# A decoder layer on one core: input also as columns, weights as blocks of 4 KB rows, token scale behind the products

## The chip, the cores and the metric

The kernel runs on one core of a Trainium2 chip. The metric is the device time in microseconds (us). The engines are TensorE (PE; PEld is its weight load), VectorE (DVE), ScalarE (ACT), GpSimd (POOL) and SyncE (SP), which here only issues transfers. L12 is line 12 of the kernel file; the changed kernel has line numbers of its own.

## The reference

One decoder layer, batch 1, S = 256 tokens, width D = 1024, in float32. Cut to what matters here:

```
h    = rms_norm(x, norm1_g)                  # x * rsqrt(mean(x*x) + 1e-6) * g, per token
proj = h @ w_in                              # 1024 x 5408: RWKV, attention, two gates
z    = z_rwkv + mu * (shift_right(z_rwkv) - z_rwkv)
y_a  = rwkv7_time_mix(z, ...)                # 8 heads of 64
y_b  = moba_attention(q, k, v)               # 8 heads of 64, causal here (one block of 256)
x    = x + (sigmoid(g_a) * (y_a @ w_branch_a) + sigmoid(g_b) * (y_b @ w_branch_b)) @ w_out
h2   = rms_norm(x, norm2_g)
x    = x + conv_ffn(h2, ...)                 # up 1024 x 5632, conv of width 3, GELU, down 2816 x 1024
```

The norm's factor per token, rs = rsqrt(mean(x*x) + 1e-6), is a scalar for each token. So it can be applied to x before a product with a weight, or to the product behind it.

## The kernel before, in words

**Products.** Every weight and every activation is split in two halves of a shorter format: hi is the rounded value (a cast), lo the rest (a subtraction). A product is the sum hi*hi + hi*lo + lo*hi, so each weight block of 1024 columns per partition makes three sets of products on PE. A block (128 x 1024 float32, 512 KB) is loaded into `raw` by SP (L254), cast to `whi` by ACT (L266), and subtracted into `wlo` by DVE (L276). There are 4 `raw`, 4 `whi` and 3 `wlo` buffers, and the next block's transfer is issued behind the subtraction that frees a `raw`. In `wst` (L304, L306, L309) the weights stand still and 256 tokens move; in `xst` (L325, L326, L329) activations stand still and 512 weight columns move.

**Order.** The first stage, `first_steps`, is written out by hand: within it each engine's instructions stand in the order of the code. The rest comes from two threads, `chain` (the RWKV recurrence) and `bulk` (projections: k, r, q, v, gates, branches), and later `att`; a loop by costs and latencies weaves them, and a scheduler sets each engine's order when the program is built. Every engine then works strictly in that order.

**First stage.** x is loaded by tokens (L85, four pieces of 256 KB). For tokens 0 to 127 (t = 0) ACT squares and sums (L415), a root (L422) and a reciprocal (L423) give rs, and DVE scales x (L434) before it is turned. Tokens 128 to 255 (t = 1) are turned unscaled. PE turns 16 squares of 128 x 128 (L427) into the PSUM tiles `xt`; ACT makes the upper halves times the gain (L446, `hh`), DVE the lower (L449, `hl`). The small vectors come as rows of 128 and are turned as well (L438, L149, L159). The first product takes blocks 0 and 1 of `w_in` (48 products, L489, tile `idle`, named after the warming products of L396 that stand in the same bank). Behind them r1 (rs of t = 1) is spread and turned (L508) into `rbc`, a 128 x 128 tile with the same row in each partition. `tl` (L515) is a narrow product with 32 columns, in four column groups, in plain float32.

**Behind the first stage.** `second(p)` (L369) multiplies the half of a product that belongs to t = 1 by `rbc`. `shift` mixes a token with the one ahead (ACT L372, then DVE L373). The chain goes on with `fold` (L595), the sigmoids of L607, a scan and exponentials; then it needs k, and later r and v. `num` scales the attention's parts of t = 1 by r1.

Of the kernel before, what the change touches and what calls it, by code (L numbers as in the profile page):

```python
# [18 lines left out]
S = 256  # L19
# [14 lines left out]
NEG = -3.0e38  # L34


def body(tc, x, positions, norm1_g, w_in, rwkv_mu, w_decay_up, decay_bias, w_aaa_up,
         aaa_bias, w_gate_up, k_k, k_a, r_k, ln_g, ln_b, q_norm_g, k_norm_g, w_branch_a,
         w_branch_b, w_out, norm2_g, w_up, conv_w, conv_b, w_down, out):
# [3 lines left out]
    with ctx:  # L43
# [45 lines left out]
        def rows(ap, n):  # L89
            return ap.rearrange("o d -> (o d)").rearrange("(n c) -> n c", c=128)  # L90


        p0 = t1("p0", (8, 128))
        p1 = t1("p1", (43, 128))
        p2 = t1("p2", (96, 128))
        mu1 = rwkv_mu[0]
        rk1 = r_k[0].rearrange("h n -> (h n)").rearrange("(n c) -> n c", c=128)

        x_sb = load_x((nc.sync, nc.sync))
        nc.scalar.dma_start(p0, rows(norm1_g, 8))  # L100
# [36 lines left out]
        par = cst.tile([128, 51], F32, name="par")  # L137
# [5 lines left out]
        rbc = cst.tile([128, 128], F32, name="rbc")  # L143
        r1 = rs[:, 1:2]

        pts = []

        def params_turned():
            pe.transpose(pts[0][:, 0:43], p1, ident[:43, :43])  # L149

        def late_params():
            pt = pts[0]
            dve.tensor_copy(par[:, 8:51], pt[:, 0:43])
# [3 lines left out]
        def mlp_params():  # L157
            pt = atp("pt")
            pe.transpose(pt[:, 0:96], p2, ident[:96, :96])  # L159
            dve.tensor_copy(cpar, pt[:, 0:96])  # L160
# [11 lines left out]
        loads, at_ = [], 0  # L172
        for r, n in ((mu1[0:1792].rearrange("(n c) -> n c", c=128), 14),
                     (rows(decay_bias, 4), 4), (rows(aaa_bias, 4), 4), (rows(k_k, 4), 4), (rows(k_a, 4), 4),
                     (rk1, 4), (rows(ln_g, 4), 4), (rows(ln_b, 4), 4)):
            loads.append((p1[at_:at_ + n], r))
            at_ += n
            if at_ == 14:
                loads.append((p1[14:15].rearrange("o (g c) -> o g c", g=4),
                              bass.AP(tensor=mu1.tensor, offset=mu1.offset + 1792, ap=[[0, 1], [0, 4], [1, 32]])))  # L180
                at_ += 1
        loads += [(wdu[0:64], w_decay_up[0]), (wdu[64:128], w_aaa_up[0]),

                  (wgu, w_gate_up[0, 0:128])]
        loads += [(wgt[32 * g:32 * g + 32], w_gate_up[0, 128:160, 128 * g:128 * g + 128]) for g in range(4)]
        for i, g in enumerate((q_norm_g, k_norm_g)):
            loads.append((gqk[:, i], bass.AP(tensor=g.tensor, offset=g.offset, ap=[[0, 128], [1, 64]])))
        gcol = cst.tile([128, 2], F32, name="gcol")
        gl = [(gcol[64 * q:64 * q + 64, i:i + 1], bass.AP(tensor=g.tensor, offset=g.offset, ap=[[1, 64], [1, 1]]))
              for i, g in enumerate((q_norm_g, k_norm_g)) for q in range(2)]  # L190
        loads.append((posi, positions[0].rearrange("(t p) -> p t", p=128)))
        loads += [(p2[0:66], conv_w[0].rearrange("w (n c) -> (w n) c", c=128)), (p2[66:88], rows(conv_b, 22)),
                  (p2[88:96], rows(norm2_g, 8))]

        def small_loads(n):
            for _ in range(n):
                nc.gpsimd.dma_start(*loads.pop(0))
# [1251 lines left out]
```

## Time and profile before

| | |
|---|---|
| three runs | 403.39, 404.11, 404.26 us (median 404.11) |
| profiled execution | 404.9 us, with a span of 403.1 us from the first to the last instruction |
| PE busy | 398.0 us, 3282 instructions |
| DVE busy | 321.8 us, 554 instructions |
| ACT busy | 234.7 us, 396 instructions |
| POOL busy | 44.4 us, 76 instructions |
| HBM read | 68.37 MB, 173 GB/s over the span with what is written |
| DMA packets | 60194, of which 50506 under 2 KB |

A busy share is an average over stages. In what follows a timeline row gives start, length, engine, line, operation, tiles and count, and in brackets the idle time before it and what ended it. A row of windows gives for one stretch the busy time and the count of each engine, the clock that the throttle granted by its records, and what the DMA moved. A chain row gives start and length of a piece of the chain that ended last.

### The profile page before, as it was taken

What the parts mean: (1) busy time and instruction counts of PE and PEld (TensorE: products, weight loads), DVE (VectorE), ACT (ScalarE), POOL (GpSimd) and SP (SyncE); (2) the same over time, 40 slices, a digit from 0 to 9 for tenths busy, and PEclk for the clock granted to TensorE, in tenths of its full rate; (3) what the DMA queues carried; (4) which work ended last, traced back from release to release, by engine and by line L of the source; (5) the groups of instructions that cost most, each with busy time, mean ns of one, the idle gap of its engine ahead of it and who ended that gap; (6) DMA issues with size and microseconds to landing.
All of it is one profiled execution on the core that took longest, in us unless ns stands there. A gap on an engine that the chain in (4) does not pass through costs nothing.

```text
span 403.1 us, 8318 instructions
## 1 busy us (share of the span) xinstructions
PE 398.0 (99%) x3282; PEld 347.9 (86%) x3282; DVE 321.8 (80%) x554; ACT 234.7 (58%) x396; POOL 44.4 (11%) x76
## 2 busy tenths in 40 slices
PE   8999999999999999999999999999999999999996
PEld 5899899888899898999888888888888888888885
DVE  4798999989667897688876897977869779687694
ACT  6899766366555795454564764545546446355450
POOL 7600505213410011100000000000000000000000
PEclk9999999999999999999999999999999999999999
DMA  7983556746844335536664657565665665656612
GB/s 246 299 269 82 138 157 210 205 132 146 224 124 142 106 88 155 167 123 206 201 179 141 210 167 232 165 206 182 198 202 167 209 193 171 209 180 198 195 54 106
DMA packets 60194, 70.36 MB, mean 175 GB/s; under 512 B 7608, under 2 KB 50506, under 8 KB 60154
## 3 DMA queue, kind: packets, MB, share of 16 engines
q1 hardware_dynamic: 59222, 69.40, 57.0%
q0 software_dynamic: 880, 0.41, 0.6%
q8 instruction: 26, 0.43, 0.5%
q14 instruction: 14, 0.11, 0.1%
q10 hardware_dynamic: 52, 0.01, 0.0%
HBM read 68.37 MB, written 1.44 MB: 173 GB/s over the span
## 4 chain that ended last, share of the span: by engine, by line
PE 98%; DMA 1%; SPq 0%; DVE 0%; issue 0%
PE acc L1330 20%; PE acc L1335 10%; PE acc L304 9%; PE acc L306 8%; PE acc L309 8%; PE acc L325 5%; PE acc L329 5%; PE acc L326 5%; PE f L1352 5%; PE f L1350 5%; PE f L1354 5%; PE idle L489 2%; PE pgr L715 1%; PE xt L427 1%; DMA x<-in_x_dram 1%; PE ppt L1155 1%
## 5 line engine op out<-in xcount | busy, mean ns | idle before, releaser
L266 ACT CAST whi<-raw 128x1024 fp32r<-128x1024 f32 x122 | 127.8, 1051 | 111.6 <-PE acc L1330 41.2
L276 DVE TENSOR_TENSOR wlo<-raw,whi 128x1024 fp32r<-128x1024 f32 x122 | 148.3, 1218 | 37.0 <-PE acc L1335 14.0
L1330 PE MATMUL acc<-hx,whi 128*128 128x512 f32 x352 | 89.5, 395 | 0.0
L1330 PEld LDWEIGHTS acc<-hx,whi 128*128 128x128 f32 x352 | 63.4, 188 | 12.4
L304 PE MATMUL acc<-hx,whi 128*128 128x256 f32 x224 | 56.3, 287 | 0.0
L306 PE MATMUL acc<-hx,whi 128*128 128x256 f32 x224 | 54.1, 278 | 0.0
L1335 PEld LDWEIGHTS acc<-hx,wlo 128*128 128x128 f32 x352 | 46.8, 188 | 4.0
L1335 PE MATMUL acc<-hx,wlo 128*128 128x256 f32 x352 | 47.3, 277 | 0.0
L304 PEld LDWEIGHTS acc<-hx,whi 128*128 128x128 f32 x224 | 42.1, 188 | 2.5 <-issue 1.4
L306 PEld LDWEIGHTS acc<-hx,whi 128*128 128x128 f32 x224 | 42.1, 188 | 0.1
L309 PE MATMUL acc<-hx,wlo 128*128 128x256 f32 x224 | 34.6, 276 | 0.0
L1352 PE MATMUL f<-whi,hb 128*128 128x512 f32 x80 | 31.2, 390 | 0.0
L1354 PE MATMUL f<-wlo,hb 128*128 128x512 f32 x80 | 31.2, 390 | 0.0
L1350 PE MATMUL f<-whi,hb 128*128 128x512 f32 x80 | 31.2, 389 | 0.0
L309 PEld LDWEIGHTS acc<-hx,wlo 128*128 128x128 f32 x224 | 29.6, 188 | 0.0
L1340 DVE TENSOR_REDUCE an<-acc 128x256 f32<-128x512 f32 x22 | 14.2, 686 | 9.4 <-PE acc L1335 9.3
L325 PE MATMUL acc<-whi,hx 128*128 128x512 f32 x48 | 19.4, 405 | 0.0
L326 PE MATMUL acc<-whi,hx 128*128 128x512 f32 x48 | 18.8, 391 | 0.0
L1354 PEld LDWEIGHTS f<-wlo,hb 128*128 128x128 f32 x80 | 15.0, 188 | 3.2
L1352 PEld LDWEIGHTS f<-whi,hb 128*128 128x128 f32 x80 | 15.0, 188 | 2.8
L1350 PEld LDWEIGHTS f<-whi,hb 128*128 128x128 f32 x80 | 15.0, 188 | 2.8
L329 PE MATMUL acc<-wlo,hx 128*128 128x512 f32 x48 | 14.9, 392 | 0.0
(341 smaller groups left out, 635.1 us busy)
## 6 DMA issues: line engine op xcount, KB each, us to landing
raw<-in_w_ffn_up_dram SPq DMA_DIRECT2D x44, 512.0 KB, 4.4
raw<-in_w_in_dram SPq DMA_DIRECT2D x41, 512.0 KB, 4.1
raw<-in_w_ffn_down_dram SPq DMA_DIRECT2D x22, 512.0 KB, 3.3
raw<-in_w_out_dram SPq DMA_DIRECT2D x8, 512.0 KB, 3.9
x<-in_x_dram SPq DMA_DIRECT2D x8, 256.0 KB, 4.2
raw<-in_w_branch_b_dram SPq DMA_DIRECT2D x4, 512.0 KB, 4.6
raw<-in_w_branch_a_dram SPq DMA_DIRECT2D x4, 512.0 KB, 3.5
out_dram<-o SPq DMA_DIRECT2D x3, 256.0 KB
```

Source lines behind the costliest of these rows:

```text
L266: act.copy(hi[:, :k * c], raw[:, :k * c])
L276: eng.tensor_tensor(lo[:, :n], raw[:, :n], hi[:, :n].bitcast(F32), op=OP.subtract)
L304: pe.matmul(om, wh[:, k, ms], xh[:, k0 + k], start=k0 + k + m == 0, stop=False, skip_group_check=True)
L306: pe.matmul(om, wh[:, k, ms], xl[:, k0 + k], start=False, stop=False, skip_group_check=True)
L309: pe.matmul(om, wl[:, k, ms], xh[:, k0 + k], start=False, stop=k0 + k == nk - 1 and m == n - 1, skip_group_check=True)
L325: pe.matmul(ps_[t], xh[:, K, ts], wh[:, k], start=K == 0, stop=False)
L326: pe.matmul(ps_[t], xl[:, K, ts], wh[:, k], start=False, stop=False)
L1330: pe.matmul(ps_[m], wh[:, k, m * 128:m * 128 + 128], hx[:, k0 + k].rearrange("p a s -> p (a s)"), start=k0 + k == 0, stop=False, skip_grou ...
L1335: pe.matmul(ps_[m][:, 0:S], wl[:, k, m * 128:m * 128 + 128], hh[:, k0 + k], start=False, stop=k0 + k == 7, skip_group_check=True)
L1350: pe.matmul(fin[f], hb[:, 0, i, ts], wh[:, 0, cs], start=st, stop=False, skip_group_check=f == 3)
L1352: pe.matmul(fin[f], hb[:, 1, i, ts], wh[:, 0, cs], start=False, stop=False, skip_group_check=f == 3)
L1354: pe.matmul(fin[f], hb[:, 0, i, ts], wl[:, 0, cs], start=False, stop=False, skip_group_check=f == 3)
```

## The change

Inputs are laid out anew on the host, without arithmetic: the weights as `blocks`, in the order in which they are used, each 128 rows of 4 KB that lie together (before, a row of a block was 4 pieces of 1 KB, 2 of 2 KB or 1 of 4 KB of the weight matrix); x a second time as columns (`x_cols`: 128 x 8 x 256, which is x turned); the small vectors as two ready 128-partition tables (`vec1`, `vec2`), and the narrow weights in one piece each.

In the first stage x is not turned, and no token's scale is applied ahead of the products. ACT squares the columns (8 squares of 128 x 256), PE sums them over the partitions with a matrix of ones, in four column groups, and a second product with 1/(32 D) adds the groups and spreads the mean to all partitions. ACT takes the root, DVE the reciprocal; `rbc` is now 128 x 256, for all tokens. `second` covers all 256 tokens, `tls` too, and `num` scales both t. rs by tokens, for `num`, comes from turning `rbc` on PE behind `fold`. GpSimd takes half of block 1's cast as well.

```diff
-        x_sb = load_x((nc.sync, nc.sync))
-        nc.scalar.dma_start(p0, rows(norm1_g, 8))
+        nc.scalar.dma_start(par, vec1)
+        xc = [b4("xc", (128, 4, S)) for _ in range(2)]
+        for ks in (slice(0, 2), slice(2, 4)):
+            nc.sync.dma_start(xc[0][:, ks], x_cols[:, ks])
...
-                for ks in ((slice(0, 2), slice(2, 4)) if first else (slice(0, k),)):
-                    nc.sync.dma_start(rv[:, ks], ap[:, ks])
+                for cs in ((slice(0, 512), slice(512, 1024)) if first else (slice(0, 1024),)):
+                    nc.sync.dma_start(raw[:, cs], blocks[i, :, cs])
...
-            v = p.rearrange("p (m c) -> p m c", m=2)[:, :, 128:256]
-            dve.tensor_tensor(v, v, rbc[:, None, :].to_broadcast([128, 2, 128]), op=OP.mult)
+            v = p.rearrange("p (m c) -> p m c", m=2)
+            dve.tensor_tensor(v, v, rbc[:, None, :].to_broadcast([128, 2, S]), op=OP.mult)
...
-            for k in range(4):
-                turn(1, k)
-            pt = bk[5][:, 256:264]
-            pe.transpose(pt, p0, ident[:8, :8])
-            dve.tensor_copy(par[:, 0:8], pt)
-            for k in (0, 1, 2, 3, 4, 6, 7, 5):
-                turn(0, k)
-            for k in (4, 6, 7, 5):
-                turn(1, k)
+            def square(k):
+                act.activation(sq[k // 4][:, k % 4], at(k), AF.Square)
...
-            for k in (0, 1, 2, 3, 4, 6, 7, 5):
+            for cs in quarters[:2]:
+                pool.tensor_copy(w[1][1][:, cs], w[1][0][:, cs])
+            lower(1, halves_[0], pool)
+            for k in range(4):
                 high(k)
-            for cs in halves_:
-                act.copy(w[1][1][:, cs], w[1][0][:, cs])
+            for k in range(4):
+                square(k)
+            for k in range(4, 8):
+                high(k)
+            act.copy(w[1][1][:, halves_[1]], w[1][0][:, halves_[1]])
+            for k in range(4, 8):
+                square(k)
...
+            first(1, 0, hh)
+            first(1, 0, hl)
+            sums = chp("sums")[:, 0:S]
+            for k in range(8):
+                g = k % 4
+                pe.matmul(sums[32 * g:32 * g + 32], tok[:, 0:32], sq[k // 4][:, k % 4], start=k < 4, stop=k >= 4,
+                          skip_group_check=True)
+            su = t1("su")
+            act.copy(su, sums)
+            first(1, 1, hh)
+            mean = chp("mean")[:, 0:S]
+            pe.matmul(mean, tok[:, 32:160], su, start=True, stop=True)
+            act.activation(rbc, mean, AF.Sqrt, bias=eps1[:, 0:1])
+            dve.reciprocal(rbc, rbc)
             act.activation(warm, eps1[:, 0:1], AF.Sigmoid)
             split_hi()
-            split_lo()
...
-            pe.transpose(pts[0][:, 128:256], rx, ident)
-            dve.tensor_copy(rbc, pts[0][:, 128:256])
...
-            dve.tensor_copy(tls[:, 0:128], tl[:, 0:128])
-            dve.tensor_tensor(tls[:, 128:256], tl[:, 128:256], rbc, op=OP.mult)
+            dve.tensor_tensor(tls, tl, rbc, op=OP.mult)
...
+            with tc.issue_after(pfi):
+                for t in range(2):
+                    pfi = pe.transpose(pft[:, S + t * 128:S + t * 128 + 128], rbc[:, t * 128:t * 128 + 128], ident).ins
+            dve.tensor_copy(rs, pft[:, S:2 * S].rearrange("p (t c) -> p t c", t=2)[:, :, 0])
```

Three places in the engines' orders, before and after. First TensorE, from behind the warming products to `tl` (`xt` are the turns, `idle` the first stage's products, `pt` small turns). Before:

```order
L427 MATMUL xt<-ident,x 128x128 x4
L438 MATMUL xt<-ident,p_69 128x8
L427 MATMUL xt<-ident,xn_168 128x128 x4
L427 MATMUL xt<-ident,xn_169 128x128 x4
L427 MATMUL xt<-ident,x 128x128 x4
L489 MATMUL idle<-hx,whi 128x256 x16
L489 MATMUL idle<-hx,wlo 128x256 x8
L149 MATMUL pt<-ident,p_70 128x43
L489 MATMUL idle<-hx,whi 128x256 x16
L489 MATMUL idle<-hx,wlo 128x256 x8
L508 MATMUL pt<-ident,rx_231 128x128
L515 MATMUL tl<-hx,wtr 32x256 x16
```

After:

```order
L410 MATMUL idle<-hx,whi 128x256 x16
L410 MATMUL idle<-hx,wlo 128x256 x8
L410 MATMUL idle<-hx,whi 128x256 x16
L425 MATMUL sums<-sq,tok 32x256 x8
L410 MATMUL idle<-hx,wlo 128x256 x8
L431 MATMUL mean<-su,tok 128x256
L441 MATMUL tl<-hx,wtr 32x256 x16
```

The turns are gone; the column sums and the mean stand among block 1's products.

Second VectorE, from the k projection's first lower half to the end of the first stage (`idle` is the first stage's product, `wlo` are lower halves). Before:

```order
L276 TENSOR_TENSOR wlo<-raw,whi 128x1024
L509 COPY rbc<-pt 128x128
L369 TENSOR_TENSOR idle<-idle,rbc 128x2x128
L373 SCALAR_TENSOR_TENSOR xwa<-idle,par,xwa 128x255
L523 COPY tls<-tl 128x128
L524 TENSOR_TENSOR tls<-tl,rbc 128x128
L373 SCALAR_TENSOR_TENSOR xg<-idle,par,xg 128x255
L276 TENSOR_TENSOR wlo<-raw,whi 128x1024
```

After:

```order
L252 TENSOR_TENSOR wlo<-raw,whi 128x1024
L433 RECIPROCAL rbc<-rbc 128x256
L317 TENSOR_TENSOR idle<-idle,rbc 128x512
L321 SCALAR_TENSOR_TENSOR xwa<-idle,par,xwa 128x255
L449 TENSOR_TENSOR tls<-tl,rbc 128x256
L321 SCALAR_TENSOR_TENSOR xg<-idle,par,xg 128x255
L252 TENSOR_TENSOR wlo<-raw,whi 128x1024 x2
```

The copy of `rbc` has become a reciprocal of 256 columns, and the rescale covers 512.

Third VectorE where k's shifts (`zk`) end and r's lower halves begin. Before:

```order
L373 SCALAR_TENSOR_TENSOR zk<-acc,par,zk 128x255
L276 TENSOR_TENSOR wlo<-raw,whi 128x1024
L373 SCALAR_TENSOR_TENSOR zk<-acc,par,zk 128x255
L369 TENSOR_TENSOR acc<-acc,rbc 128x2x128
L276 TENSOR_TENSOR wlo<-raw,whi 128x1024
```

After:

```order
L321 SCALAR_TENSOR_TENSOR zk<-acc,par,zk 128x255
L317 TENSOR_TENSOR acc<-acc,rbc 128x512
L252 TENSOR_TENSOR wlo<-raw,whi 128x1024
L321 SCALAR_TENSOR_TENSOR zk<-acc,par,zk 128x255 x2
L252 TENSOR_TENSOR wlo<-raw,whi 128x1024
```

k's second rescale (`acc<-acc,rbc`) moves ahead of the lower half of r's second block.

More of the change, by code (lines that the diff above doesn't have):

```diff
@@ L87, in load_x @@
             return xs
[L89 to L97, printed above, removed]
[L99 to L100 removed]
+        par = cst.tile([128, 51], F32, name="par")
+        nc.scalar.dma_start(par, vec1)
+        xc = [b4("xc", (128, 4, S)) for _ in range(2)]
+        for ks in (slice(0, 2), slice(2, 4)):
+            nc.sync.dma_start(xc[0][:, ks], x_cols[:, ks])
         first_low = []
@@ L142, in body @@
         rs = cst.tile([128, 2], F32, name="rs")
[L143 to L149, printed above, removed]
+        rbc = cst.tile([128, S], F32, name="rbc")
         def late_params():
-            pt = pts[0]
-            dve.tensor_copy(par[:, 8:51], pt[:, 0:43])
             dve.tensor_scalar(omm, par[:, MU:MU + 15], -1.0, 1.0, op0=OP.mult, op1=OP.add)
             dve.tensor_scalar(omka, par[:, KA:KA + 4], -1.0, 1.0, op0=OP.mult, op1=OP.add)
[L157 to L160, printed above, removed]
         def col(i):
@@ L378, in first_steps @@
         def first_steps():
-            for _ in range(2):
-                nc.scalar.dma_start(*loads.pop(0))
             for i in range(2 * NRAW):
                 load_next(i == 0, early=i >= NRAW)
+                if i == 0:
+                    nc.sync.dma_start(xc[1], x_cols[:, 4:8])
                 if i == 2:
-                    nc.sync.dma_start(wtr, win[:, :, 1792:1824])
+                    nc.sync.dma_start(wtr, w_narrow)
                 if i == 3:
-                    for _ in range(2):
-                        nc.sync.dma_start(*loads.pop(7))
+                    nc.sync.dma_start(wdu, w_two_up)
             skipped[0] = NRAW
@@ L474, in first_steps @@
                 lower(0, cs, dve)
-            lower(1, halves_[0], pool)
-            for k in (4, 6, 7):
+            for k in range(4, 8):
                 low(k)
-            square(1, 1)
-            low(5)
             lower(1, halves_[1], dve)
-            root(1)
-            rx = t1("rx1", (128, 128))
-            dve.tensor_copy(rx, r1.to_broadcast([128, 128]))
+            late_params()
             def first(b, lo_, xx, ks=(0, 1, 2, 3)):
@@ L1222, in bulk @@
             yield from proj4("k", 4)
-            for _ in range(7):
-                nc.sync.dma_start(*loads.pop(0))
+            nc.sync.dma_start(wgu, w_gate)
+            nc.sync.dma_start(wgt, w_gate_rest)
+            nc.sync.dma_start(gqk, gain_rows)
             yield from proj4("r", 0)
@@ L1243, in bulk @@
             threads.insert(1, ["att", attention(), now_t + 3.0])
-            for _ in range(3):
-                nc.sync.dma_start(*loads.pop(0))
+            nc.sync.dma_start(cpar, vec2)
             for j in range(1, 4):
@@ L1438 @@
     arrays, args = {}, []
-    for name in _INS:
-        a = np.ascontiguousarray(inputs[name])
+    for name, a in lay_out(inputs).items():
+        a = np.ascontiguousarray(a)
         arrays[f"in_{name}_dram"] = a
```

160 lines of the change are left out of this document (61 added, 99 removed).

## The prediction

> **What bounds the kernel now.** I read the page first (busy shares, the chain of waits), then TensorE's own waits, then the first 20 us engine by engine, then how far ahead of TensorE the other engines run.
>
> ```profile
> PE 398.0 (99%) x3282; PEld 347.9 (86%) x3282; DVE 321.8 (80%) x554; ACT 234.7 (58%) x396; POOL 44.4 (11%) x76
> PE 98%; DMA 1%; SPq 0%; DVE 0%; issue 0%
> PE idle L396 <- DVE eps L391: 1.5, 1, 1.5
> PE xt L427 <- DMA x<-in_x_dram: 0.4, 1, 0.4
> ```
>
> The chain that ends last is TensorE for 98% of the span, and TensorE waits twice in all: 1.5 us at the start and 0.4 us for x. So no weight transfer is ever waited for there, and what the change can give lies in the first 18 us, where TensorE works on turns, or in fewer products later (there are none). What it can take is a new wait.
>
> ```profile
> 1.46 3.60 PE L396 MATMUL idle<-ones 128*128 128x512 bf16 x8 [1.46 <-DVE eps L391]
> 5.50 1.09 PE L427 MATMUL xt<-ident,x 128*128 128x128 f32 x4 [0.45 <-DMA x<-in_x_dram]
> 6.72 1.97 PE L427 MATMUL xt<-ident,xn 128*128 128x128 f32 x8
> 9.20 2.86 PE L489 MATMUL idle<-hx,whi 128*128 128x256 f32 x16
> 11.89 1.07 PE L489 MATMUL idle<-hx,wlo 128*128 128x256 f32 x8
> 13.08 2.10 PE L489 MATMUL idle<-hx,whi 128*128 128x256 f32 x16
> 16.13 1.93 PE L515 MATMUL tl<-hx,wtr 128*32 128x256 f32 x32
> 17.99 0.38 PE L304 MATMUL acc<-hx,whi 128*128 128x256 f32 x1
> ```
>
> (Timeline of TensorE: start, length, line, tiles, count.) Turns run from 5.50 to about 9.2, the first stage's 48 products from 9.20 to 16.1, the narrow product `tl` to 18.0, then the k projection starts. Here is what makes the turns cheaper than they look:
>
> ```profile
> 9.00:10.00 1.00, 0.81 (x4) 0.88 (x5) 1.00 1.10 375
> 10.00:11.00 1.00, 1.00 (x7) 1.00 (x7) 1.00 1.22 276
> 11.00:12.00 1.00, 1.00 (x11) 1.00 (x10) 1.00 1.23 225
> 205.50 0.54 PE xt L1291 x4
> ```
>
> Of line 489 alone, 0.81 us hold 4 products before 10 us (0.20 each), 11 fit into the microsecond from 11 to 12. Four turns take 1.09 us at 5.5 and 0.54 us at 205.5 (chain of waits). TensorE thus runs at about half pace (0.21 us for 256 columns) until some 10.8 us and at 0.113 (from 8 in 1.07, whose last alone lasts about 0.28) after that, though the clock column says 1.00 throughout. The 3.7 us of turns are worth about 1.9 us at full pace.
>
> **The change part by part.**
>
> *The start of the products.* Block 0's first half stood fifth among the quarter megabytes in SP's queue; now it is third, behind two pieces of the columns.
>
> ```profile
> 1.65 3.72 DMA x<-in_x_dram
> 8.11 1.43 POOL L466 CAST whi<-raw 128x256 fp32r<-128x256 f32 x4 [1.31 <-DMA raw<-in_w_in_dram]
> 7.24 3.34 ACT L446 ACTIVATE hx<-xt,par 128x256 fp32r<-128x256 f32 x8 [0.95 <-PE xt L427]
> 10.45 1.15 ACT L470 CAST whi<-raw 128x512 fp32r<-128x512 f32 x2
> ```
>
> The third piece landed at 1.65 + 3.72 = 5.4. One GpSimd quarter (1.43/4 = 0.36, with hand-over 0.4) gives the first product at 5.8 instead of 9.2. ScalarE's upper halves cost 0.42 each as before (3.34/8) and are ready by then.
>
> *The work up to the end of the token sums.* Let M be the moment the token means stand in PSUM. TensorE has 48 products, 8 column-sum products in fp32 (half of `tl`'s 1.93: 0.96) and one fp32 product with 256 columns, priced by the fold below at 0.59. Four changes of kind cost 0.12 each, as from the end at 12.96 to the next start at 13.08: 0.5.
>
> ```profile
> 19.48 0.59 PE L595 MATMUL fold<-tls,fold 128*128 128x256 f32 x2
> ```
>
> If the pace changes at 10.8 as before: 5.0/0.21 = 24 products until then, 24 x 0.113 = 2.7 after, so M = 10.8 + 2.7 + 0.96 + 0.59 + 0.5 = 15.6. If it changes by 7.5, block 1 sets it: it lies at the same place (2 MB) in the queue as before, where the row of line 470 shows it landed by 10.45; with 1 us less than that, M is about 14.5. If it changes at 12.3: 31 products until then, 17 x 0.113 after, M = 16.3. I take 15.4, nearest the first with some weight on the early case. [...]
>
> *From the sums to the shifts.* Before, `rbc` was at hand soon after block 1; now a root and a full reciprocal precede it, on ScalarE and VectorE, and every rescale (`second`) covers 256 tokens, not 128.
>
> ```profile
> 16.23 0.29 DVE L509 COPY rbc<-pt 128x128 f32<-128x128 f32 x1 [1.26 <-PE pt L508]
> 16.56 0.43 DVE L369 TENSOR_TENSOR idle<-idle,rbc 128x256 f32<-128x256 f32 x1
> 18.43 0.45 ACT L372 ACTIVATE xg<-idle,omm 128x256 f32<-128x256 f32 x1
> 43.33 1.75 DVE L650 RECIPROCAL rq<-rq 128x256 f32<-128x256 f32 x1
> 42.89 0.41 ACT L649 ACTIVATE rq<-rq 128x256 f32<-128x256 f32 x1
> 39.03 0.68 DVE L638 TENSOR_TENSOR wgl<-wgu,wgh 128x512 fp32r<-128x512 f32 x1
> ```
>
> Old path from 16.23 to the xg shift: 2.20. New: minus the copy (0.33) plus root 0.41, reciprocal 1.75, hand-overs 0.15, and 0.68 - 0.43 = 0.25 for the wider rescale (priced by the nearest 512-wide row): 4.4. The xg shift starts at M + 4.4 = 19.8, against 18.43: 1.4 us later, although TensorE is up to 1 us ahead.
>
> *Where that delay goes.* Behind the xg shift ScalarE is full, and its next goods are upper halves.
>
> ```profile
> 20.11 0.47 ACT L372 ACTIVATE xgt<-fold,omm 128x256 f32<-128x256 f32 x1 [0.28 <-PE fold L595]
> 31.56 1.04 ACT L266 CAST whi<-raw 128x1024 fp32r<-128x1024 f32 x1
> 32.63 1.23 DVE L276 TENSOR_TENSOR wlo<-raw,whi 128x1024 fp32r<-128x1024 f32 x1 [0.46 <-ACT whi L266]
> 20.00:35.00 15.00, 15.00 (x132) 14.53 (x132) 12.43 (x37) 14.86 (x26) 0.00 (x0) 1.00 0.58 185
> 35.00:60.00 25.00, 25.00 (x175) 21.88 (x174) 24.79 (x32) 19.38 (x31) 5.85 (x14) 1.00 0.56 149
> 57.30 1.23 DVE L276 TENSOR_TENSOR wlo<-raw,whi 128x1024 fp32r<-128x1024 f32 x1
> 58.78 0.62 PE L309 MATMUL acc<-hx,wlo 128*128 128x256 f32 x4
> ```
>
> (Windows: the busy times are PE, PEld, DVE, ACT, POOL.) From 20 to 35 ScalarE is busy 14.86 of 15 us; VectorE then starts r's second lower half at 32.63, the moment the cast ends, and is busy 24.79 of 25 us until 60. At its end v's second block: lower half ready at 58.53, used at 58.78. VectorE runs 0.25 us ahead of TensorE there, the smallest lead I found anywhere. So the sum is VectorE's. The same ScalarE items as before stand between the xg shift and that cast; the old 0.28 idle before L372 goes: 1.4 - 0.28 = +1.1. In VectorE's order k's second rescale now precedes this lower half (before, it followed), so it starts some 0.1 behind the cast: +1.2. From there to v's second lower half stand the same rows, without that rescale (-0.33) and with r's two rescales wider (+0.5): +0.2. Lower half ready: 58.53 + 1.2 + 0.2 = 59.9, that is 1.15 us after TensorE used it before. In case of a gap in VectorE's run (it waits for ScalarE's shifts and the root of `rq`) up to 0.5 more; with M = 14.5, 0.25 us late; with M = 16.3, 2.0 us.
>
> Until then TensorE's lead does not help: it is spent as one wait of 1 to 2 us at v's second block.
>
> *Behind it.* The leads are larger; one of the smallest:
>
> ```profile
> 176.34 1.22 DVE L276 TENSOR_TENSOR wlo<-raw,whi 128x1024 fp32r<-128x1024 f32 x1
> 180.84 0.39 PE L309 MATMUL acc<-ybh,wlo 128*128 128x256 f32 x2
> 176.89 0.25 PE L159 MATMUL pt<-ident,p 96*128 96x96 f32 x1
> ```
>
> 180.84 - 177.56 = 3.3 us cover the wider rescales of v and the gates, 10 x 0.25 = 2.5 us over 110 us; without that cover they would cost up to 2.5. One turn (L159) goes: -0.1. The two turns of `rbc` (2 x 0.14) and the narrower small loads lie ahead of v's wait and cost nothing by themselves; without the wait they would take back 0.3. Rows of 4 KB instead of 1 KB: nothing, since TensorE waits for no weights, and 1 KB rows already moved 375 GB/s (row of 9 to 10 us).
>
> Sum: 403.1 + 1.15 - 0.1 = 404.2 of span. The profiled execution took 404.9 for 403.1, the median is 404.11, so I put the +1.05 on the median: 405.2.
>
> **The rivals.** (1) *Even*: full pace comes early, M near 14.5. VectorE then has v's half 0.25 late, less the L159 turn: +0.1, 404.2. For it: the pause before the first product (5.1 to 5.8) is short, and some 3 us of dense products follow it. Against: after a pause of 0.45 at the same place the old kernel stayed slow until 10.8. (2) *TensorE's lead survives*: VectorE is not the bound at v's block, because its stretch holds slack that I take for work, or the reciprocal lies beside a wait. Then the k projection's start counts: M + 0.2 + 1.75 = 17.3 against 17.99, +0.3 for the two turns, -0.1: -0.5 with M = 15.4, -1.4 with 14.5; 403.0 for the middle. Against it: 24.79 of 25 us. (3) *VectorE does not recover*: the wider rescales after 60 us use up the 3.3 us of lead; from the point where their sum and the 1.2 us pass it, each costs 0.25. With half of the ten uncovered: 405.2 + 1.25 = 406.5. (4) *The layout alone does nothing*: the 4 KB rows show in the DMA's landing times and nowhere else. It is part of each case.
>
> **How the numbers follow.** Forecast 0.55, with its own range 404.6 to 406.2 (M from 14.8 to 16.0 and up to 0.5 of gaps); rival 1 0.22, rival 2 0.16, rival 3 0.07. A measurement of this kernel cannot tell less than 0.2% (0.8 us) from no change. Of the forecast a quarter lies under +0.8, of rival 1 nearly all, of rival 2 a quarter: same 0.14 + 0.20 + 0.04 = 0.38; faster 0.02 + 0.12 = 0.14; slower 0.41 + 0.07 = 0.48. Range 403.5 to 406.5.
>
> **What would show it.** Right: the first product of block 0 near 5.8 at about 0.21 apart; the means' root near 15.5; a 1.75 us reciprocal right behind; the xg shift near 19.8; the cast of r's second block ending near 33.7; a wait of TensorE for VectorE's lower half near 59, 1 us or more with what k's earlier start gained, and none behind it. Wrong: no TensorE wait around 59 (rival 2), the pace doubling before 8 us (rival 1), further waits for lower halves after 70 us (rival 3), or a TensorE wait for the sums or for the first stage's data between 6 and 15 us, which I have at nothing.

## The result, and the profile after

The changed kernel took 409.88 us (median of 4 runs, 409.0 to 410.2); the kernel before took 403.89 (median of 4). The ratio is 1.0148, 95% interval 1.0132 to 1.0163: 6.0 us slower. The forecast was 405.2 with a range up to 406.5; the direction was right, the size was not. The profiled execution took 409.75 for a span of 407.66; before, it took 404.9 for 403.13. So 4.5 us of span lie between the two, and 0.3 us outside the span. The remaining 1.1 us or so is that the profiled execution of the kernel before (404.9) lay 1.0 above its own median, and that of the changed kernel 0.1 below.

The page: busy times, the chain of waits, and then TensorE's waits.

```profile
PE 399.6 (98%) x3282; PEld 348.7 (86%) x3282; DVE 327.0 (80%) x546; ACT 234.4 (58%) x395; POOL 40.2 (10%) x68
PE 79%; DVE 8%; ACT 6%; DMA 5%; issue 1%; SPq 0%; ACTq 0%; DVEq 0%
PE idle L410 <- POOL whi L384: 2.0, 1, 2.0
PE idle L343 <- DVE eps L337: 1.5, 1, 1.5
PE acc L283 <- DVE wlo L252: 0.9, 1, 0.9
```

TensorE held 98% of the chain before, now 79%: from 21.6 to 61.6 us the chain runs over ScalarE and VectorE, and what lies ahead of that is put down to transfers (5%). Two new waits stand in the list: 2.0 us for block 0's upper half, and 0.9 for a lower half. The second is v's second block, the place that the prediction named:

```profile
60.37 1.23 DVE L252 TENSOR_TENSOR wlo<-raw,whi 128x1024 fp32r<-128x1024 f32 x1
61.64 0.74 PE L283 MATMUL acc<-hx,wlo 128*128 128x256 f32 x4 [0.94 <-DVE wlo L252]
```

The first stage on TensorE (timeline: start, length, line, tiles, count):

```profile
7.05 3.78 PE L410 MATMUL idle<-hx,whi 128*128 128x256 f32 x16 [2.00 <-POOL whi L384]
12.34 2.23 PE L410 MATMUL idle<-hx,whi 128*128 128x256 f32 x16
14.49 1.07 PE L425 MATMUL sums<-sq,tok 128*32 128x256 f32 x16
16.55 0.59 PE L431 MATMUL mean<-su,tok 128*128 128x256 f32 x2
18.93 0.39 PE L278 MATMUL acc<-hx,whi 128*128 128x256 f32 x1
```

First product at 7.05 (forecast 5.8), means in PSUM at 16.55 + 0.59 = 17.14 (forecast 15.4), the k projection at 18.93 (before 17.99). Of line 410 alone, in windows of one microsecond:

```profile
12.00:13.00 1.00, 1.00 (x7) 1.00 (x7) 1.00 1.07 422
13.00:14.00 1.00, 1.00 (x11) 1.00 (x10) 1.00 1.01 406
```

Seven products per microsecond up to 13, then eleven: here full pace came at about 12.8, against 10.8 before.

Behind the means, ScalarE and VectorE:

```profile
17.18 0.47 ACT L432 ACTIVATE rbc<-mean,eps 128x256 f32<-128x256 f32 x1 [1.09 <-PE mean L431]
17.67 1.28 ACT L434 ACT_TABLE_LOAD   x1
17.68 1.75 DVE L433 RECIPROCAL rbc<-rbc 128x256 f32<-128x256 f32 x1 [3.34 <-ACT rbc L432]
19.07 1.03 ACT L242 CAST whi<-raw 128x1024 fp32r<-128x1024 f32 x1
19.54 0.70 DVE L317 TENSOR_TENSOR idle<-idle,rbc 128x512 f32<-128x512 f32 x1
20.27 0.47 ACT L320 ACTIVATE xwa<-idle,omm 128x256 f32<-128x256 f32 x1 [0.17 <-DVE idle L317]
21.62 0.45 ACT L320 ACTIVATE xg<-idle,omm 128x256 f32<-128x256 f32 x1
34.33 1.04 ACT L242 CAST whi<-raw 128x1024 fp32r<-128x1024 f32 x1
```

Root, reciprocal, rescale, shift, as forecast; but from 17.67 to 20.10 ScalarE is not idle either: it loads the Sigmoid table, warms up and casts k's second block. That row had not been in the prediction, and it comes up again below.

**Where the 4.5 us of span lie.** Comparing when TensorE begins the same piece of work in both traces: +0.94 at the start of the k projection; +1.54 at the second lower half of k (0.28 of it the two turns of `rbc`, 0.3 a wait at the fold, which needs `tls` and so the factors); +1.76 at 43 us; +2.86 at v's second lower half (61.64 against 58.78); then a slow drift up to +4.2 where the last stage begins, with no wait to be seen; nothing in the last stage; and 0.3 at the very end, behind the last product (3.46 to 3.54 us in every trace with the first stage of the change, 3.20 to 3.21 in those without; why was not looked for). That the last stage itself costs nothing, its rows say: the same line before (first fence) and after (second), with the duration of one (least, median, most) and the first and last start.

```profile
L1350 PE MATMUL f<-whi,hb x80: 389/389/393, 239.8 to 393.6; 128*128 128x512 f32 x80
```

```profile
L1275 PE MATMUL f<-whi,hb x80: 389/389/393, 244.0 to 397.8; 128*128 128x512 f32 x80
```

Both begin and end 4.2 apart. The drift of 1.35 between 61 and 244 us has a trace of its own. The same products of the branch of `yb`, before and after:

```profile
L309 PE MATMUL acc<-ybh,wlo x32: 276/276/284, 172.3 to 182.5; 128*128 128x256 f32 x32
```

```profile
L283 PE MATMUL acc<-ybh,wlo x32: 281/281/283, 175.8 to 186.3; 128*128 128x256 f32 x32
```

Each product lasts 276 ns before and 281 after, and the starts follow each other at 113.3 ns before and at 117.8 after. Counted over all neighbouring starts in the whole trace, 161 steps of 116 to 120 ns stood beside 1044 of 111 to 115 before; after, it is 485 beside 697. I call them long steps below. 324 more of them at 4.5 ns are 1.46 us; 273 of the 324 lie between 61 and 244 us, and their 1.23 us are nearly all of the drift of 1.35 there.

The theory at this point: (a) the first transfers and the half pace put the means 1.7 us late; (b) VectorE and ScalarE hand that on to v's second block, by the chain of the prediction; (c) the long steps add about 1.4; (d) 0.3 at the end. Rivals: the 4 KB rows do some of it; the reciprocal alone does (b); the long steps come from where the tiles lie in memory.

### The profile page after: what moved, and what is told of

It is laid out like the page before. It is cut to its first block, busy times and chain, and to the rows that moved or that the text cites. A ratio compares the mean times of both kernels' runs of the same rounds, so it can differ in the third digit from the quotient of the medians.

```text
span 407.7 us, 8269 instructions
## 1 busy us (share of the span) xinstructions
PE 399.6 (98%) x3282; PEld 348.7 (86%) x3282; DVE 327.0 (80%) x546; ACT 234.4 (58%) x395; POOL 40.2 (10%) x68
## 4 chain that ended last, share of the span: by engine, by line
PE 79%; DVE 8%; ACT 6%; DMA 5%; issue 1%; SPq 0%; ACTq 0%; DVEq 0%
PE acc L1255 20%; PE acc L1260 10%; PE acc L278 5%; PE acc L283 5%; PE acc L280 5%; PE f L1277 4%; PE f L1275 4%; PE f L1279 4%; PE acc L299 4%; PE acc L300 4%; PE acc L303 4%; DMA raw<-in_blocks_dram 3%; DVE wlo L252 2%; ACT whi L242 2%; DMA gqk<-in_gain_rows_dram 2%
## 5 line engine op out<-in xcount | busy, mean ns | idle before, releaser
L1260 PE MATMUL acc<-hx,wlo 128*128 128x256 f32 x352 | 47.3, 277 | 0.0
L283 PE MATMUL acc<-hx,wlo 128*128 128x256 f32 x224 | 35.6, 280 | 0.9 <-DVE wlo L252 0.9
```

Source lines behind the costliest of these rows:

```text
L283: pe.matmul(om, wl[:, k, ms], xh[:, k0 + k], start=False, stop=k0 + k == nk - 1 and m == n - 1, skip_group_check=True)
L1260: pe.matmul(ps_[m][:, 0:S], wl[:, k, m * 128:m * 128 + 128], hh[:, k0 + k], start=False, stop=k0 + k == 7, skip_group_check=True)
```

## The experiments

All times below are medians of runs beside runs of the kernel before on the same chip; the ratio to it is what compares between groups. "Means" is the end of the product that puts the token means into PSUM, "v ready" the end of v's second lower half on VectorE. Chips, and so the runs beside which a ratio stands, differ between groups; "vectors later" has two runs, "columns apart" three.

| run | us | ratio (95%) | first product | means | v ready | long steps |
|---|---|---|---|---|---|---|
| kernel before | 403.89 | 1 | 9.20 | | 58.53 | 161 |
| changed kernel | 409.88 | 1.0148 (1.0132 to 1.0163) | 7.05 | 17.14 | 61.59 | 485 |
| the same again | 410.42 | 1.0152 (1.0128 to 1.0176) | 7.61 | 16.60 | 61.05 | 454 |
| layout only | 404.72 | 1.0007 (0.9996 to 1.0017) | 8.69 | | 58.17 | 172 |
| twelve warm products | 408.93 | 1.0119 (1.0092 to 1.0146) | 7.16 | 15.61 | 60.04 | 503 |
| no reciprocal | 409.80 | 1.0131 (1.0098 to 1.0165) | 7.40 | 17.59 | 61.76 | 471 |
| fast root | 408.43 | 1.0101 (1.0076 to 1.0125) | 7.64 | 16.82 | 60.05 | 472 |
| vectors later | 409.80 | 1.0136 (1.0102 to 1.0169) | 8.29 | 17.34 | 61.78 | 598 |
| columns apart | 408.02 | 1.0089 (1.0060 to 1.0118) | 5.63 | 14.24 | 58.67 | 442 |
| turn back | 409.02 | 1.0119 (1.0094 to 1.0144) | 7.33 | 16.42 | 60.87 | 461 |
| before, moved | 404.87 | 1.0012 (0.9998 to 1.0027) | 8.96 | | 57.97 | 143 |
| after, moved | 409.31 | 1.0130 (1.0109 to 1.0151) | 7.26 | 16.32 | 60.77 | 435 |
| combined | 406.53 | 1.0065 (1.0043 to 1.0087) | 6.32 | 15.53 | 58.75 | 448 |
| breaks | 409.66 | 1.0160 (1.0132 to 1.0187) | 7.39 | 16.48 | 60.92 | 519 |

### The same kernel again

> The changed kernel once more, unaltered. Theory: the loss of 5.9 us has four parts: the k projection starts 0.94 us later (first product at 7.05, full pace only at 12.8), some 0.6 us of turns and a wait at the fold behind it, one wait of about 1.1 us for VectorE near 61, and products of 256 columns that start 117.8 ns apart instead of 113.3 in 485 steps instead of 161 (1.5 us). If the two distances are a matter of the program, this run has 450 to 520 long steps again and the same time, 409.9 within 0.5. Rival: they are an accident of one execution; then the count differs by 100 or more from 485 and the span moves along by 4.5 ns for each. In both cases the first product starts near 7.0.

410.42 and 454 long steps, at nearly the same places: the long steps belong in the main to the program, they were no accident of one execution. But the first product came half a microsecond later (7.61), the means half a microsecond earlier (16.60), and the clock did something else. Windows over this trace, the sixth column of numbers (behind the busy times) being the granted clock:

```profile
4.50:7.90 3.40, 0.64 (x4) 0.30 (x3) 1.76 (x4) 2.93 (x8) 1.02 (x3) 1.00 0.96 360
7.90:11.30 3.40, 3.40 (x18) 3.40 (x18) 3.07 (x6) 2.65 (x8) 2.28 (x5) 0.50 1.04 411
11.35:13.00 1.65, 1.65 (x17) 1.65 (x16) 1.65 (x2) 1.65 (x4) 1.61 (x3) 1.00 1.04 403
```

Full clock was already granted at 4.5, in the warm-up products (the eight took 3.38 us here, 3.60 in the first execution). In the next 3.4 us TensorE was busy for only 0.64, since it waited for block 0 (2.77 us); then the granted clock was 0.50 for 3.4 us, in which TensorE was busy throughout and did 18 products, and 1.00 again from 11.3, where the next 1.65 us held 17. So in this execution the pause before the first product was paid for a second time, in the 3.4 us from 7.9.

### The blocks of 4 KB rows alone

```diff
-                ap = queue.pop(0)
-                k, c = ap.shape[1], ap.shape[2]
+                i, k, c = queue.pop(0)
...
-                    nc.sync.dma_start(rv[:, ks], ap[:, ks])
+                    nc.sync.dma_start(raw[:, cs], blocks[i, :, cs])
```

(on the kernel before, with the same blocks as in the change and nothing else)

> The kernel before, with nothing changed but the weights, given as blocks of 4 KB rows. Theory: 404.0 within 0.5, TensorE's two waits as before, blocks land no later. Rival 1 (rows of 4 KB land later at the start, as the first ones did in the changed kernel): the first product starts 0.5 us or more later and the time is 405 or more. Rival 2 (the blocks' rows bring the 117.8 ns steps): more than 300 such steps, 404.8 or more.

404.72 against 404.62 beside it, 1.0007 (0.9996 to 1.0017), 172 long steps: the time is as the theory had it. Both rivals fall, since the long steps hardly grew in number and the first product came at 8.69, 0.5 earlier than in the kernel before. TensorE's waits were not "as before": besides the two there are three more of 0.3 to 0.6 us, in a trace in which full clock came at 4.9 us instead of 10.9. Its lead of 0.36 us over the kernel before stood until 90 us and was gone by 111. So the layout of the weights neither helps nor harms the time here, and an early clock was worth nothing to the kernel before in this trace.

### Warm-up without a pause

```diff
-            keep_warm(8)
+            keep_warm(12)
```

> Twelve products of the ones tile instead of eight at the start, so that TensorE has no pause between 5.1 and 6.9 us. Theory (the half pace until 12.8 comes from the pause before the first stage): full pace by 9 us at the latest, the means in PSUM near 15 instead of 17.1, the k projection begins near 16.9 instead of 18.9, VectorE's wait near 60 stays at about 1.1 because both engines move together: 407.9. Rival 1 (the pace changes by a clock of its own): nothing moves, 409.9. Rival 2 (the first stage is bound by transfers and casts, not by TensorE): full pace early, but the means no more than 0.7 us earlier, 409.2.

Full clock came at 4.35 and stayed:

```profile
8.00:11.00 3.00, 2.91 (x22) 2.49 (x20) 2.71 (x6) 2.12 (x5) 1.64 (x3) 1.00 1.03 410
```

22 products in 3 us, where the unaltered run did 18 in 3.4. The means came at 15.61, 1.0 to 1.5 us earlier than without, and the median fell by 1.5 us (1.0119 against 1.0152, with intervals that overlap): less than the forecast 2.0, because with TensorE at full pace the first stage begins to wait for block 1 (GpSimd's cast of it starts at 10.16, when it lands). So the clock accounts for 1 to 1.5 us at the means. Rival 1 falls, and rival 2 holds in part. The wait for VectorE stayed at 0.9, as both engines moved together.

### Without the reciprocal

```diff
             act.activation(rbc, mean, AF.Sqrt, bias=eps1[:, 0:1])
-            dve.reciprocal(rbc, rbc)
```

> The reciprocal of the token factors (1.75 us on VectorE) is left out, so the first stage's results are scaled by the root itself; all other work is the same. Theory (VectorE's lateness is the reciprocal): the xg shift starts 1.7 us earlier, the gap before the fold goes (0.3), and the wait near 61 goes (1.1): 408.5. Rival (VectorE waits for ScalarE in that stretch, or TensorE's own start decides): the wait near 61 stays above 0.7, and the time is 409.6 or more.

409.80: here the theory failed. ScalarE's row of this run:

```profile
17.63 0.47 ACT L432 ACTIVATE rbc<-mean,eps 128x256 f32<-128x256 f32 x1 [1.09 <-PE mean L431]
18.12 1.28 ACT L434 ACT_TABLE_LOAD   x1
19.53 1.03 ACT L242 CAST whi<-raw 128x1024 fp32r<-128x1024 f32 x1
20.47 0.46 ACT L320 ACTIVATE xwa<-idle,omm 128x256 f32<-128x256 f32 x1
```

From root to xwa shift it is 2.84, against 3.09 with the reciprocal: 1.75 us of VectorE's work were worth 0.25. The shift waits for whichever is later, the rescaled sums or ScalarE itself, and ScalarE has the table load (1.28), a warm-up call (0.2) and a cast (1.03) in its own order behind the root. Both rows were equally long. The wait near 61 was still 0.6, in two parts: the time is the rival's, the wait lies between the two forecasts.

### One function for the factors, and a cast moved ahead

```diff
-            act.activation(rbc, mean, AF.Sqrt, bias=eps1[:, 0:1])
-            dve.reciprocal(rbc, rbc)
+            act.activation(rbc, mean, AF.Abs_reciprocal_sqrt, bias=eps1[:, 0:1])
...
             su = t1("su")
+            split_hi()
             act.copy(su, sums)
...
             split_lo()
-            split_hi()
             return xwa, xg, tls
```

> The changed kernel with the root and the reciprocal as one ScalarE function (its table is loaded by the first warm-up call instead of the root's), and with one cast of an upper half moved ahead of the copy of the sums, where ScalarE stands idle 2.8 us, so that each later cast comes one place earlier. Theory, as the run without the reciprocal left it (behind the root ScalarE's own row of table load 1.28, warm-up 0.2 and cast 1.03 is as long as VectorE's reciprocal, so that removing one alone gains nothing): the xwa shift starts 2.1 us behind the means instead of 3.1, the cast of r's second block ends 15.5 us or less behind the k projection's start instead of 16.4, and the wait near 61 falls under 0.3: 409.2 against 410.4. Rival 1 (VectorE's row after 34 us alone sets that wait): the wait stays at 0.7 or more. Rival 2 (the delay is at the transfers): the shifts do not start earlier.

The wait for VectorE is gone; these are all waits of TensorE that are left:

```profile
PE idle L410 <- POOL whi L384: 2.9, 1, 2.9
PE idle L343 <- DVE eps L337: 1.5, 1, 1.5
```

The cast of r's second block ended 16.65 behind the means instead of 18.23, v's second lower half was ready 43.23 behind them instead of 44.45, and the ratio fell from 1.0152 to 1.0101. Counted from the k projection, as the expectation had it, the cast came no earlier (17.35 behind, against 15.5 forecast), but that start is no measure here: TensorE's order changed too, and k's first product (16.12) now stands ahead of the means. The xwa shift came only 2.87 behind the means, not 2.1: the cast behind the table load still stood there, since the one taken out was the last. What had to be shortened was ScalarE's queue behind the root as a whole. Since three things changed at once (the function, the place of a cast, TensorE's order), their shares are not told apart.

### What slows the first transfers

Two runs for one question. The first moves the load of the 51 vectors:

```diff
-        nc.scalar.dma_start(par, vec1)
...
                 if i == 0:
+                    nc.sync.dma_start(par, vec1)
                     nc.sync.dma_start(xc[1], x_cols[:, 4:8])
```

> The changed kernel with the load of the 51 vectors (128 rows of 204 bytes) moved from the start of ScalarE's queue to SP's queue, behind the first block's two halves. Theory A (these small rows hold up the first transfers, which move 150 to 160 GB/s from 1.5 to 3.5 us against 255 before): 230 GB/s or more in that time, the first half of block 0 lands by 5.7 instead of 6.4 to 7. Theory B (the pieces of x's columns, 2 KB out of rows of 8 KB, do it): no change there, and the upper halves start 1 us later, because they wait for the vectors.

The second gives x's columns as three inputs, so that no piece is cut out of longer rows:

```diff
-            nc.sync.dma_start(xc[0][:, ks], x_cols[:, ks])
+            nc.sync.dma_start(xc[0][:, ks], x_lo[ks.start // 2])
...
-                    nc.sync.dma_start(xc[1], x_cols[:, 4:8])
+                    nc.sync.dma_start(xc[1], x_hi)
```

> The changed kernel with the first two pieces of x's columns and the second half given as three inputs of their own, so that each piece is one stretch of memory instead of 2 KB out of every 8 KB. Theory B: 230 GB/s or more from 1.5 to 3.5 us, the first product at 6.2 instead of 7.05 to 7.6. Theory A: no change, first product at 7.0 or later.

The first 2 us of transfers, in four traces (the last two numbers are the mean busy share of the DMA engines and GB/s): before, changed, vectors later, columns apart.

```profile
1.50:3.50 2.00, 2.00 (x5) 0.70 (x6) 0.00 (x0) 1.02 (x1) 1.94 (x6) 1.00 0.74 255
```

```profile
1.50:3.50 2.00, 2.00 (x5) 0.69 (x6) 0.10 (x1) 1.16 (x2) 1.42 (x4) 1.00 0.60 160
```

```profile
1.50:3.50 2.00, 2.00 (x5) 0.69 (x6) 0.10 (x1) 0.72 (x2) 1.42 (x4) 1.00 0.65 186
```

```profile
1.50:3.50 2.00, 2.00 (x5) 0.69 (x6) 0.10 (x1) 1.16 (x2) 1.42 (x4) 1.00 0.70 236
```

It was mainly the columns: with pieces of 2 KB cut out of every 8 KB the transfers ran at 160 GB/s (135 to 160 in the eight traces with this start), with the same pieces in one stretch at 236 (232 in the run at the end; x itself, 2 KB out of 4 KB, 255). The vectors' small rows account for about a third (186 without them), and moved behind, they hold up the upper halves (first product 8.29). With the columns apart, TensorE:

```profile
5.63 2.62 PE L410 MATMUL idle<-hx,whi 128*128 128x256 f32 x16 [0.58 <-POOL whi L384]
13.65 0.59 PE L431 MATMUL mean<-su,tok 128*128 128x256 f32 x2
16.04 0.39 PE L278 MATMUL acc<-hx,whi 128*128 128x256 f32 x1
```

First product at 5.63 behind a pause of 0.58 us, 16 products in 2.62 us instead of 3.78, with full clock from 4.9 on; means at 14.24, k projection at 16.04, 2.9 earlier than in the changed kernel and 1.95 earlier than before the change. By the ratios, 1.0089 against 1.0148 to 1.0152, this gives back some 2.5 us. The profiled execution was the fastest of three (406.88; median 408.02), so what the others lost besides is not shown. In it, VectorE's wait at v stayed at 0.9 and the long steps stayed (442): an early start alone is not what decides.

### The long steps: a turn put back, and the tiles moved

```diff
+                    if c == 3: pe.transpose(atp("pt")[:, 0:96], ident[:96], ident[:96, :96])
                     p = chp("pc")
```

> The changed kernel with one turn of 96 rows put back on TensorE, where the kernel before turned the last parameters (its result is not used). Theory (which distance a stretch of products takes, 113.3 or 117.8 ns, is set by the phase in which it is entered): the stretch of 143 long steps behind this place, or others behind it, change: the count of long steps moves by more than 100 from the 454 and 485 seen, and the time by 4.5 ns for each step, down to 409.7 if the stretch becomes short. Rival (the distance hangs on the tiles' places in memory or on the transfers): the count stays within 40 of that, the time within 0.3 of 410.4.

461 long steps, the stretch from 181 us on unchanged: the removed turn is not what brought them, and a shift of the entry by 0.1 us does not change the stretch. The median of 409.02 is below that of the changed kernel, but the intervals of the two ratios overlap, and this is about what the first stage varies by (means at 16.3 to 17.6 us in the six traces that leave the work up to them alone). Its profiled execution was an outlier (412.26) that shows the clock's price once more. TensorE waited 1.3 us for a transfer at about 106, and from 107 to 110.5 the granted clock was 0.53 on average:

```profile
105.00:107.00 2.00, 0.94 (x63) 0.93 (x64) 1.67 (x2) 0.58 (x1) 1.10 (x2) 1.00 0.92 57
107.00:110.50 3.50, 3.50 (x10) 2.70 (x9) 0.00 (x0) 0.00 (x0) 0.00 (x0) 0.53 0.93 341
```

Next, the places of the tiles. The wider factor tile pushed hx, the halves and the branches' outputs up by 512 bytes. The kernel before was given the same shift, and the changed kernel the old places:

```diff
-        rbc = cst.tile([128, 128], F32, name="rbc")
+        rbc = cst.tile([128, 256], F32, name="rbc")[:, 0:128]
```

> The kernel before, with nothing changed but 512 unused bytes per partition behind the tile of the token factors, so that the inputs of the products (hx, the weights' halves and all that follows them) lie 512 bytes higher, exactly where the changed kernel has them. Theory (the places of the tiles decide which distance the products of 256 columns take): more than 350 long steps (117.8 ns) instead of 161, and 0.9 to 1.5 us more, 405.4. Rival (the distance hangs on the timing with which a stretch is entered): 161 within 40 and the time of the kernel before, 404.3 within 0.4.

```diff
-        rbc = cst.tile([128, S], F32, name="rbc")
+        rbc = sb.tile([128, S], F32, name="rbc", tag="rbc", bufs=1)
+        tokm = cst.tile([128, 128], F32, name="tokm")
```

> The changed kernel with its wide factor tile kept elsewhere and a 512-byte tile in the old place, so that hx, the weights' halves and the branches' outputs lie exactly where the kernel before has them; instructions and their order are the same. Theory (places): fewer than 280 long steps instead of 454 to 485, and about 1 us less than the changed kernel, 409.0. Rival (timing of entry): 440 to 500 long steps and 409.9 to 410.4.

143 and 435 long steps: each kernel keeps its own, wherever the tiles lie. The theory of places falls. The time of the second, 409.31, lies nearer the theory's 409.0 than the rival's 409.9, but its interval overlaps that of the changed kernel, and it is the count that decides.

### The long steps: breaks

```diff
             for j in range(4):
                 p = acc()
+                if br == 0 and j: pe.transpose(chp("pt")[:, 0:96], ident[:96], ident[:96, :96])
                 yield from wst(p, 2, yh, yl)
```

> The changed kernel with one turn of 96 rows (result not used) ahead of the second, third and fourth quarter of the last branch product, which run in the stretch of 143 long steps from 181 to 198 us. Theory (each break lets the products fall into either distance anew): at least one of the three stretches behind the turns runs at 113.3 ns, and the count of long steps falls by 40 or more, to under 430. Rival (something that lasts through that time holds the distance long): all three stay long, the count is within 25 of 454 to 485. Each turn costs 0.1 to 0.2 us, so the time says little: 410 within 0.6.

The products of the two branches, first the end of the branch of `yb`, which has no break, then that of `ya` with its three turns:

```profile
L283 PE MATMUL acc<-ybh,wlo x9: 281/281/281, 182.8 to 185.6; 128*128 128x256 f32 x9
L283 PE MATMUL acc<-yah,wlo x28: 276/276/283, 186.7 to 195.7; 128*128 128x256 f32 x28
```

The stretch of long steps from 180 us, 143 in the runs before, ended after 70 at the first turn (188.6); three or so steps behind each turn were still long, and all three stretches that followed ran at 276 ns a product. So nothing that lasts through that time holds the distance long: here a stretch kept its distance until a turn broke it. Not every break does so. In the changed kernel two other turns, in the row below, have long steps ahead of them and behind them:

```profile
180.56 0.38 PE L899 MATMUL pc<-ident,yc 128*128 128x128 f32 x2
```

The count did not fall, it rose to 519, because another stretch, from 24 to 40 us, took the long distance for 132 steps in this execution. In the profile of the changed kernel the same products, with the same places and shapes, were short, as this pair shows (changed kernel, then the run with the vectors later, where that stretch was long as well):

```profile
L283 PE MATMUL acc<-hx,wlo x35: 276/276/384, 24.5 to 35.7; 128*128 128x256 f32 x35
```

```profile
L282 PE MATMUL acc<-hx,wlo x43: 277/281/388, 24.7 to 39.2; 128*128 128x256 f32 x43
```

What decides at the entry was not found: the products ahead of a long and of a short stretch were the same, down to a few ns in their distances.

### All that helped, together

The columns apart, the one function, the cast moved ahead, one warm-up product more, and the tiles in the old places.

> All that helped put together: x's columns as three inputs of their own, one ScalarE function for the token factors, a cast moved ahead of the copy of the sums, one more warm-up product, and the tiles in the places of the kernel before. Theory: first product at 5.6 to 5.9, no wait for VectorE near 60 (0.9 less than with the columns alone) and none at the fold (0.3): 406.8 from the 408.0 of the columns alone; if the tiles' places decide the distances, another 1.2 less: 405.6. Rival (something behind the first stage gives the early start back): a wait of TensorE of 0.7 or more behind 40 us, and 407.5 or more.

406.53, 1.0065 (1.0043 to 1.0087): about 3.4 us of the 6.0 regained, but not faster than the kernel before. The first product was forecast at 5.6 to 5.9 and came at 6.32, since block 0's first half landed only at 5.69; and full clock came at 10.0 us, not at 4.9 as with the columns alone. So the means stood at 15.53 and not at 14.24:

```profile
6.32 3.78 PE L411 MATMUL idle<-hx,whi 128*128 128x256 f32 x16 [0.84 <-POOL whi L385]
```

What TensorE waits for:

```profile
PE idle L344 <- DVE eps L338: 1.5, 1, 1.5
PE idle L411 <- POOL whi L385: 0.8, 1, 0.8
PE acc L284 <- DVE wlo L253: 0.2, 1, 0.2
```

Against the kernel before, TensorE is 0.36 us ahead from 24 to 38 us, 0.2 to 0.4 behind at 62 to 68 (0.2 of wait, and long steps), 0.55 behind from 107 to 150, and 1.42 behind from 219 on: what is left in this trace is mostly long steps (448; 269 more than before between 61 and 244 us, 1.2 us). The rival (a wait of 0.7 or more) did not come.

## Why the prediction was wrong, step by step

**The first product at 5.8: wrong, 7.05 to 7.6.** The step that failed was the landing of the third piece, priced by a piece of x (3.72 from issue to landing). In the change it took 6.44 - 1.65 = 4.8 us in the profiled execution. I had looked at the size and the place in the queue, both equal, and not at the rows from which the pieces are cut. The run with the columns apart shows it: 5.63. (With all that helped it was 6.32, so half a microsecond and more is left to chance.)

**The moment of full pace, 10.8: wrong, 12.8 in the profiled execution, 11.3 in the next.** That it would stay at 10.8, between the 7.5 and the 12.3 set beside it, was my estimate, made with the first product fixed at 5.8; no run shows that the moment stays. It is no property of the kernel from which to take 10.8: by the clock's records full clock came at 10.9 in the kernel before, but at 4.9 with only the layout changed and at 6.3 with only the tiles moved, and from 4.3 to 13.4 in the traces of the changed first stage, partly to be taken back. The formula for the means was right: with the two measured inputs, (12.8 - 7.05)/0.21 = 27 products, 21 x 0.113 = 2.4, and 12.8 + 2.4 + 0.96 + 0.59 + 0.5 = 17.25, measured 17.14. Both inputs are outside the bounds from which I drew M (14.5 to 16.3). With the first product at 7.05 and the pace still at 10.8 the formula gives 16.3, so the transfer is worth 0.7 us and the later pace 1.0. This is the largest error: 17.14 - 15.4 = 1.74 us in this execution, and 0.9 to 2.2 over the six traces with this first stage (16.3 to 17.6).

**From the means to the xg shift, 4.4: right in size, 21.62 - 17.14 = 4.48, but only half understood.** The reciprocal was named as what sets it. ScalarE's table load, warm-up and cast are as long, which the run without the reciprocal shows (0.25 gained of 1.75). Both must go for either to be worth something. That 4.4 came out is in part luck: the row that was left out happened to be as long as the one that was counted. My step counted ScalarE's items behind the xg shift and left out those ahead of it.

**From there to v's second lower half: right.** The cast of r's second block was to end 33.7 - 15.4 = 18.3 behind the means; it ended 35.37 - 17.14 = 18.23 behind. The lower half was to be ready 59.9 - 15.4 = 44.5 behind; measured 44.45. This holds in the other runs too: 61.05 - 16.60 = 44.45, with twelve warm products 60.04 - 15.61 = 44.43, with the columns apart 58.67 - 14.24 = 44.43, and 44.44 or 44.45 in four more; without the reciprocal it is 44.17, and only where ScalarE's queue was shortened as well is it 43.2 (fast root, combined). So every microsecond by which the means are late arrives at v's second block undiminished, and TensorE's start is not what counts there: the forecast +1.15 and the 1.74 of the means give 2.89, and TensorE began that half 61.64 - 58.78 = 2.86 later. The wait itself was 0.94 and not 1 to 2 us, since TensorE had no lead to spend: it was 1.76 us late itself by 43 us. The rival that TensorE's lead survives falls; the run with the columns apart, 1.95 ahead at the k projection and only level at v, is its clearest refutation. Rival 1 (even) is what the first 60 us of that run were, with means at 14.24 and v ready at 58.67 against 58.53.

**Behind v nothing: wrong by 1.35 us.** Its terms held: no wait followed in the profiled execution, the wider rescales stayed covered, the 4 KB rows did nothing (1.0007). (Four other traces show a wait of 0.2 to 0.4 us for a small transfer, `X`, between 103 and 106 us, the one with the turn put back 1.5 in all; the sum had no term for that.) What the sum lacked was a term for the long steps: I took the products that are not touched to run at the same distance as before. The moved tiles, the layout and the breaks show what it is not and how it behaves; why the changed program enters more of its stretches with the long distance stays open.

**The two turns of `rbc` cost nothing: right while v's wait stood.** They and the fold's wait (0.58) lie ahead of it.

**The sum on the median.** The profiled executions differ by 409.75 - 404.9 = 4.85; made up of 2.9 at v, 1.35 of drift, 0.3 at the end and 0.3 outside the span. The rest up to 6.0 is the place of the profiled execution of the kernel before among its runs. I had seen that it lay high (404.9 against 404.11), and put the forecast difference on the median as if the profiled execution of the changed kernel would lie as high above its own; it lay 0.1 below.

The range was too narrow for a plain reason: the forecast's own upper end (406.2) came from a bound on the pace and on gaps, with the transfer ahead of it held as known; the stated end (406.5) is rival 3's time; and neither left anything for products that start further apart.

## What to carry to other kernels

When a transfer is replaced by one of the same size in another layout, price it by a row with the same cut (length of a piece against the distance of its rows; here 160 GB/s against 236), and let what comes behind it, the moment of full clock included (10.8 in the sum, 12.8 and 11.3 measured), start from both ends of that bound. Where a wait of one engine is taken out, list what stands in the order of the next engine over the same time: a stall that two rows of equal length cause is not cured by shortening one (here 1.75 us less gave 0.25). And follow lateness on the engine that is full, not on the one that is fast: here 1 us at the means was 1 us at v's second block, whatever TensorE had gained by then.

## What the hardware showed that I had not expected

- With pieces of 2 KB cut out of 8 KB rows the transfers from 1.5 to 3.5 us ran at 135 to 160 GB/s, with the same bytes in one stretch at 232 and 236.
- Where full clock had come during the warm-up products and a pause of 2.3 to 3.2 us followed them, the granted clock was 0.50 for the whole 3.4 us behind it, though TensorE was busy throughout those (18 products in the second run, 16 with the fast root). Behind a pause of 1.53 us (twelve warm products) and of 0.58 (columns apart) it stayed at 1.00. With a wait of 1.3 us at 106 us, in a stretch where TensorE was busy 0.94 of 2 us, it was 0.53 from 107 to 110.5. The pause alone does not tell: in the 3.4 us ahead of a halving TensorE was busy for 0.2 to 1.1 us (five traces) and 1.86 (the wait at 106 us); with 1.88 (twelve warm products) and 2.76 (columns apart) the clock stayed. What sets the moment is not shown.
- Products of 256 columns stood mostly at two distances in these traces, 113.3 and 117.8 ns, kept over up to 140 steps (kernel before) and 143. The places are the same from run to run in much of the program and differ in some stretches; in the run with breaks a turn of 96 rows in between ended a long stretch after 70 steps instead of 143. With some 300 more of the long ones the changed kernel loses 1.2 to 1.4 us that no list of waits shows.
